# Buffers and load distances around a retention stage: three tiles for weight sums, longer prefetch, two shuffle tiles, masked keys on ScalarE

## The chip, the cores and the metric

The kernel runs on one core of one Trainium2 chip. The metric is the device time of one execution in microseconds (us); the number given for a kernel is the median of its runs. TensorE is called PE here (PEld is its weight load), VectorE DVE, ScalarE ACT, GpSimd POOL, and SyncE SP. SP computes nothing in this kernel; it issues the loads, in the order of its queue. POOL computes a little and issues the stores and a few loads.

## The reference

One step of a one-layer decoder over 1024 prompt tokens and 8 x 4 sample tokens, all in float32. The parts that matter here are the combined input projection, the retention branch with four heads, and its gate and output projection.

```python
h = xn @ w_in
q_a, k_a, v_a, q_r, k_r, v_r, gate_r, gm_a, gm_r = jnp.split(h, split_points(), axis=-1)
...
qr = rope_ret(q_r.reshape(B, T, N_HEADS_R, DK_R).astype(jnp.float32), pos)
kr = rope_ret(k_r.reshape(B, T, N_HEADS_R, DK_R).astype(jnp.float32), pos) * (DK_R ** -0.5)
o_r, new_s = retention(qr, kr, vr, ret_s0.astype(jnp.float32))
y_r = (jax.nn.silu(gate_r) * head_rms(o_r)) @ w_r_proj
mixed = (jax.nn.sigmoid(gm_a) * y_a + jax.nn.sigmoid(gm_r) * y_r) @ w_o
x = x + rms_norm(mixed, g_post_mix)
f, new_conv = conv_ffn(rms_norm(x, g_pre_ffn), conv_ctx, w_up, conv_w, conv_b, w_down)

def retention_chunk(q, k, v, s0, log_g):     # one block of 128 tokens (4 for a sample row)
    scores = jnp.einsum('bihd,bjhd->bhij', q, k) * dmask[None]
    inner = jnp.einsum('bhij,bjhe->bihe', scores, v)
    cross = jnp.einsum('bihd,bhde->bihe', q, s0) * q_decay[None, :, :, None]
    s_new = (jnp.exp(log_g * L)[None, :, None, None] * s0
             + jnp.einsum('bjhd,bjhe->bhde', k * k_decay[None, :, :, None], v))
    return inner + cross, s_new
```

## The kernel before

Every float32 product is made of three matmuls on a high and a low part of each operand (`mm3`, L254 to L257). The high part is a copy by ACT (L228, L329), the low part a subtraction by DVE (L223, the line of the helper `ew`, through which most of DVE's arithmetic goes). The large products use a seven-product scheme on 2 x 2 blocks, so that sums of weight blocks have to be made: by DVE for the input weights in `in_split`, and, for two later matrices, ahead of their use in `quad_sums`, which loads a piece of `w_down` or `w_r_proj` into a tile `zt`, makes four sums in place and stores the tile to DRAM (`s_d`, `r_d`).

The stage that the change touches lies at about 270 to 740 us. Its backbone is `stream()`, a generator that runs 16 pairs of column blocks of the input projection through PE (PSUM tiles `ps_q`), each pair in two halves of tokens (`j`), each half of seven products of 12 matmuls. Between the products other work is put in by hand, by `adv(n)`, which lets the stream run n products further:

- **The sample part**, about 320 to 455 us: `sample(h)` for the four heads. For each pair of sample rows it loads a state `s0`, splits it (`s0s`), multiplies the keys by a mask of one row (`kb`, L1039, two for each pair of rows, 32 in all) and updates the state. In the same time `post_qk` turns q and k of the heads by their angles: a shuffle on DVE into a tile `sh` (L822), a product on POOL, a product and a sum (all L223 or L225).
- **The prompt part**, about 455 to 715 us: 32 blocks of retention (4 heads of 8 blocks). `ahead(g)` issues the loads of q and k (`qk`, by SP, L1089) and of v (`vt`, by POOL, L1096) of a later block and makes the block's scores (`front`, L1118, L1119). `middle` multiplies by v and moves the state on (L1131 to L1138), `tail` multiplies by the gate, and in the first three blocks of each head calls `quad_sums`; in blocks 4 and 7 `z_sums` makes four sums of the gated result into another `zt` tile. `post_ga` loads a `zt` tile too (L838).

The tiles `zt` are two and turn around between these three users; the weights of a pair lie in two tiles `w_raw` of three, two in a pool `wraw` and one in a pool `wsum`. A tile whose turn comes again makes its writer wait until the last use of its old content has ended. A scheduler sets the order on each engine when the program is built; each engine and each queue then works in that order.

Of the kernel before, what the change touches and what calls it, by code (L numbers as in the profile page):

```python
# [120 lines left out]
def trunk(ctx, tc, I, O):  # L121
# [95 lines left out]
    def f32(ap):  # L217
        return ap.bitcast(F32)
# [63 lines left out]
        G.tensor_tensor(out=rs[:r, :c], in0=ms[:r, :c], in1=mhalf[:r, :c], op=ALU.pow)  # L282
        return rs[:r, :c]

    def quad_sums(w, d, m, pt, kk, q, eng=None):
        eng = eng or V


        q = q[:, :, :2 * P]
        for u in range(2):  # L290
            r0, c0 = 1024 * pt + 512 * kk, (m + 4 * u) * P
            pin(ld.dma_start(out=q[:, :, u * P:u * P + P],
                             in_=w[r0:r0 + 512, c0:c0 + P].rearrange("(k p) n -> p k n", p=P)))
        a11, a12, a21, a22 = (q[:, r::2, u * P:u * P + P] for u in range(2) for r in range(2))
        ew(eng, a22, a21, a22, add)
        ew(V, a21, a11, a21, sub)
# [4 lines left out]
    def down_sums(n, q, eng=None):  # L301
        quad_sums(w_down, s_d, n // 6, n // 2 % 3, n % 2, q, eng)

    def quad_weights(raw, w, d, p, c, pt):

# [511 lines left out]
    def post_qk(h):  # L817
        def post(j, o):
            c, d = (t[:, 2 * HW * j:2 * HW * (j + 1)] for t in (rcos, rsin))
            for i in range(2):  # L820
                sh, x = ST("sh", (P, 2 * HW)), both(o)[:, i]
                V.stream_shuffle(sh, x, R_SHUF)  # L822
# [4 lines left out]
        return post  # L827

    def post_gate(h):
        def post(j, o):  # L830
            S.activation(o, o, AF.Silu)
            st.dma_start(out=of_half(gr_d[h], j), in_=both(o))
        return post

    def post_ga(m):
        def post(j, o):
            y = ST("zt", (P, T), bufs=2)
            ld.dma_start(out=both(y), in_=of_half(gm_d[m:m + 2], j))  # L838
            S.activation(o, o, AF.Sigmoid)
            ew(V, o, o, y, mult)  # L840
            st.dma_start(out=of_half(a_d[m:m + 2], j), in_=both(o))
        return post

    def post_gm(m):
        def post(j, o):
            st.dma_start(out=of_half(gm_d[KD + m:KD + m + 2], j), in_=both(o))
        return post
# [8 lines left out]

    def in_split(n):

        a11, a12, a21, a22 = pair_weights(w_in, *pairs[n][:2])
        yield  # L860
        s1 = wx["sum"].tile([P, 4, P], F32, name="s1")
        yield w_split(a11, V)
        ew(V, s1, a21, a22, add)
        yield w_split(s1, V)
        ew(V, s1, s1, a11, sub)
        yield w_split(s1, V)
        yield w_split(a12, V)
        ew(V, a12, a12, s1, sub)
        yield w_split(a12, V)
        ew(V, a21, a11, a21, sub)  # L870
        yield w_split(a21, V)
        yield w_split(a22, V)

    def stream():

        early = (A11, S1, S2, A12, S4, S3)
        ws = in_split(ORDER[0])
        next(ws)
        ops = {p: next(ws) for p in early}
        coming = in_split(ORDER[1])  # L880
# [2 lines left out]
        for i, n in enumerate(ORDER):  # L883
            for j in range(2):
# [17 lines left out]
                for p in (A11, S1, A22, S2, A12, S4, S3):  # L902
                    if p == A22:
                        if last is not None:
                            product(A22, *last)
                        if j == 0:
                            ops[A22] = next(ws)
                            ws = coming
                        if last is not None:
                            yield  # L910
                        continue
                    if p == S2:
                        if nh < 2:
                            TE.matmul(bk[1], ops[p][:, 0], xop(ex1, p, j, 0)[0], start=True, stop=True)
                            S.copy(out=bk[1], in_=bk[0])
                        nh += 1
                    product(p, bk[{A11: 0, A12: 0, S2: 1, S3: 1, S1: 2, S4: 2}[p]], ops[p], j, dst)
                    if p == A11 and nh >= 2:
                        S.copy(out=bk[1], in_=bk[0])
                    if p == S4:  # L920
                        V.tensor_tensor(out=c12, in0=bk[2], in1=c12, op=add)
                    if p == S3:
                        V.tensor_tensor(out=c22, in0=bk[1], in1=c22, op=add)
# [9 lines left out]
                PEND.append((pairs[n][2], j, o))  # L933
            if i + 1 < len(ORDER):
                ops = nxt
        product(A22, *last)
# [53 lines left out]
    def load_s0(n):  # L990
        if n >= 2 * DB:
            return
        h, bb = n // 4, 2 * (n % 4)
        s0s_[n] = ST("s0", (P, 2, 256), bufs=3)
        ld.dma_start(out=s0s_[n], in_=I["state_ret"][0, bb:bb + 2, h].rearrange("b k e -> k b e"))

    def sample(h):
        gS = float(GAMMA[h] ** 4)
        dm = ST("dm", (P, P))
        ld.dma_start(out=dm, in_=I["dmask"][:, h, 1])  # L1000
        qk8 = ST("qk8", (P, 2, NS), bufs=2)
# [24 lines left out]
        TE.matmul(po, h8[:, 0, 0:2 * NS], v8, start=True, stop=False)  # L1026
        for bb in range(0, DB, 2):
            s0 = s0s_[(h * DB + bb) // 2]
            load_s0((h * DB + bb) // 2 + 1)
# [6 lines left out]
            pk = ps_a()  # L1036
            for b in range(2):
                kb = ST("kb", (P, P), F32R, bufs=2)
                V.tensor_scalar(out=kb, in0=f32(h8)[:, 1], scalar1=bm[:, bb + b:bb + b + 1],  # L1039
                                scalar2=None, op0=mult)  # L1040
                TE.matmul(pk[:, 256 * b:256 * b + 256], kb, v8, start=True, stop=True)
            V.scalar_tensor_tensor(out=s0, in0=s0, scalar=gS,
                                   in1=pk.rearrange("p (b e) -> p b e", b=2), op0=mult, op1=add)
# [102 lines left out]
    def tail(g, pt, o):  # L1146
# [3 lines left out]
        while a < NS + P * tt + P:  # L1150
# [561 lines left out]
```

## Time and profile before

| | |
|---|---|
| Median of 3 runs | 1695.76 us (1694.22 to 1698.17) |
| Profiled execution, its own time | 1696.89 us |
| Its span, first to last instruction | 1695.1 us |
| Mean granted clock of PE | 0.993 |
| PE busy | 1637.6 us |
| DVE busy | 1227.7 us |
| ACT busy | 852.1 us |
| POOL busy | 485.2 us |

The times run from the span's start. A matmul's row in the profile is longer than its turn, as matmuls overlap, so a PE that is busy all the time is only a PE without gaps. In a row of groups stand the line, the engine, the operation, the tile written and those read, the count, then the busy time, the mean time of one in ns, and the idle time of the engine just before them with what ended it. In a row of waits stand the waiting engine and line, what it waited for, the total in us, how many times, and the longest. In a row of stretches stand, for each engine, the busy time and the number of instructions, and then the granted clock of PE (1.00 is full), the busy share of the DMA engines and GB/s.

### The profile page before, as it was taken

How to read it: one execution, taken by the hardware profiler on the slowest of the kernel's cores; microseconds unless marked ns; L12 is line 12 of the kernel's file. 1: busy time of each engine (PE TensorE's matmuls, PEld its weight loads, DVE VectorE, ACT ScalarE, POOL GpSimd, SP SyncE). 2: the span in 40 equal slices, each digit the busy share in tenths (PEclk: the TensorE clock that was granted, in tenths of full speed). 3: DMA queues.
4: the chain of work that ended last, by engine and by line, in shares of the span. 5: the costliest groups of instructions: out<-in, count | busy, mean ns of one | idle time of the engine just before them, and what ended most of it. 6: DMA issues, size and time to landing. Idle time of an engine off the chain costs nothing.

```text
span 1695.1 us, 32482 instructions
## 1 busy us (share of the span) xinstructions
PE 1637.6 (97%) x12551; PEld 1593.2 (94%) x12551; DVE 1227.7 (72%) x2067; ACT 852.1 (50%) x1858; POOL 485.2 (29%) x686
## 2 busy tenths in 40 slices
PE   8999999888989999999999999999999999999997
PEld 7999989887979999999778999999999999999997
DVE  7887737798545666557756888888888888445576
ACT  6566534444545554454432555555555556443343
POOL 4242420455233433232311123222222323111102
PEclk9999999999999999999999999999999999999998
DMA  7212222444666777497722245444444447866654
GB/s 197 66 45 73 80 76 103 138 144 146 218 200 198 243 233 248 156 294 223 227 98 83 69 132 158 146 154 149 157 156 145 145 146 251 251 185 201 199 170 160
DMA packets 273291, 273.88 MB, mean 162 GB/s; under 512 B 23041, under 2 KB 234273, under 8 KB 273122
## 3 DMA queue, kind: packets, MB, share of 16 engines
q1 hardware_dynamic: 239377, 155.25, 31.6%
q0 software_dynamic: 33760, 116.57, 19.8%
q8 instruction: 98, 1.61, 0.4%
q14 instruction: 56, 0.45, 0.1%
HBM read 184.24 MB, written 87.49 MB: 160 GB/s over the span
## 4 chain that ended last, share of the span: by engine, by line
PE 62%; DMA 5%; DVE 4%; issue 3%; ACT 1%; POOL 1%; SPq 0%; DVEq 0%; POOLq 0%; ACTq 0%
PE ps_m L257 9%; PE ps_m L255 9%; PE ps_m L256 9%; PE ps_t L256 8%; PE ps_t L255 7%; PE ps_t L257 7%; PE ps_q L255 3%; PE ps_q L257 3%; PE ps_q L256 3%; DMA zt<-in_w_down 1%; DMA a_in<-a_d 1%; PE ps_b L1131 1%; DMA qk<-qk_d 1%; PE ps_a L1135 0%; PE ps_t L459 0%
## 5 line engine op out<-in xcount | busy, mean ns | idle before, releaser
L255 PE MATMUL ps_q<-xh,w 128*128 128x264 f32 x512 | 153.2, 299 | 9.4 <-ACT pair L900 6.2
L223 DVE SCALAR_TENSOR_TENSOR w_lo<-w_raw,w_hi 128x1024 fp32r<-128x1024 f32 x83 | 104.4, 1264 | 61.8 <-ACT w_hi L228 57.6
L255 PE MATMUL ps_t<-xh,w_hi 128*128 128x264 f32 (+2 forms) x524 | 148.9, 284 | 0.0
L256 PE MATMUL ps_t<-xl,w_hi 128*128 128x264 f32 (+2 forms) x524 | 148.7, 284 | 0.0
L257 PE MATMUL ps_t<-xh,w_lo 128*128 128x264 f32 (+2 forms) x524 | 148.0, 283 | 0.0
L256 PE MATMUL ps_q<-xl,w 128*128 128x264 f32 x512 | 147.2, 288 | 0.0
L257 PE MATMUL ps_q<-xh,w 128*128 128x264 f32 x512 | 146.5, 287 | 0.0
L257 PE MATMUL ps_m<-xh,w_lo 128*128 128x264 f32 x512 | 145.5, 285 | 0.7 <-DVE w_lo L223 0.7
L255 PE MATMUL ps_m<-xh,w_hi 128*128 128x264 f32 x512 | 145.9, 285 | 0.0
L256 PE MATMUL ps_m<-xl,w_hi 128*128 128x264 f32 x512 | 145.5, 284 | 0.0
L223 DVE SCALAR_TENSOR_TENSOR w<-w_raw,w 128x512 fp32r<-128x512 f32 x152 | 106.7, 707 | 36.1 <-ACT w L329 33.6
L1462 DVE SCALAR_TENSOR_TENSOR c_out<-u_ext,fconst,c_out 128x1024 f32<-128x1024 f32 x96 | 121.8, 1280 | 2.6 <-ACT c_out L1458 0.5
L228 ACT CAST w_hi<-w_raw 128x1024 fp32r<-128x1024 f32 x62 | 65.2, 1051 | 100.8 <-PE ps_t L256 73.6
L255 PEld LDWEIGHTS ps_q<-xh,w 128*128 128x128 f32 x512 | 97.6, 191 | 11.8 <-ACT pair L900 6.8
L329 ACT CAST w<-w_raw 128x512 fp32r<-128x512 f32 x152 | 93.8, 621 | 28.3 <-DVE w_raw L223 13.2
L257 PEld LDWEIGHTS ps_t<-xh,w_lo 128*128 128x128 f32 x524 | 98.7, 188 | 0.0
L256 PEld LDWEIGHTS ps_t<-xl,w_hi 128*128 128x128 f32 x524 | 98.6, 188 | 0.0
L255 PEld LDWEIGHTS ps_t<-xh,w_hi 128*128 128x128 f32 x524 | 98.6, 188 | 0.0
L256 PEld LDWEIGHTS ps_q<-xl,w 128*128 128x128 f32 x512 | 97.6, 191 | 0.6
L257 PEld LDWEIGHTS ps_q<-xh,w 128*128 128x128 f32 x512 | 97.2, 190 | 0.1
L257 PEld LDWEIGHTS ps_m<-xh,w_lo 128*128 128x128 f32 x512 | 96.3, 188 | 1.1 <-DVE w_lo L223 1.0
L255 PEld LDWEIGHTS ps_m<-xh,w_hi 128*128 128x128 f32 x512 | 96.3, 188 | 0.2
(448 smaller groups left out, 6059.9 us busy)
## 6 DMA issues: line engine op xcount, KB each, us to landing
w_raw<-in_w_up SPq DMA_DIRECT2D x48, 512.0 KB, 4.3
w_raw<-in_w_in SPq DMA_DIRECT2D x42, 512.0 KB, 4.3
w_raw<-s_d SPq DMA_DIRECT2D x60, 256.0 KB, 3.8
t_d<-t POOLq DMA_DIRECT2D x24, 528.0 KB, 3.9
t<-t_d POOLq DMA_DIRECT2D x24, 528.0 KB, 5.2
t<-in_w_down SPq DMA_DIRECT2D x40, 256.0 KB, 4.6
s_d<-t POOLq DMA_DIRECT2D x20, 512.0 KB, 3.5
w_raw<-in_w_down SPq DMA_DIRECT2D x36, 256.0 KB, 5.7
```

The lines of the kernel that those rows point to most:

```text
L223: pinned(V.scalar_tensor_tensor(out=out, in0=in0, scalar=1.0, in1=in1, op0=mult, op1=op))
L228: pinned(S.copy(out=hi, in_=src))
L255: TE.matmul(ps, wh, xh, start=start, stop=False, **kw)
L256: TE.matmul(ps, wh, xl, start=False, stop=False, **kw)
L257: TE.matmul(ps, wl, xh, start=False, stop=stop, **kw)
L329: S.copy(out=t[:, 0:4], in_=src)
L1131: TE.matmul(po, sT, vt, start=True, stop=tt == 0)
L1462: V.scalar_tensor_tensor(out=c[:, NS:], in0=u[:, g, NU + t:NU + t + SEQ], scalar=sc[t], in1=c[:, NS:], op0=mult, op1=add)
```

## The change

Six things are done:

1. `quad_sums` is cut in two. `quad_load` issues the loads of a piece in the `tail` of blocks 0, 1 and 2 of a head; the sums and the store are made in the `tail` of the block after (1, 2 and 3). The tiles `zt` become three. `post_ga` issues its load as soon as a half is ready and not when its other work is done.
2. `qk` is loaded 4 blocks ahead into 5 tiles (2 ahead into 3 before), `vt` 3 ahead into 5 (2 into 4), the states `s0` 2 ahead into 4 (1 into 3).
3. `post_qk` has two shuffle tiles and makes both shuffles first.
4. The masked keys `kb` are made on ACT.
5. The third `w_raw` tile leaves the pool `wsum`: in the sample part the weights have two tiles, in the prompt part again three. The two loads of a pair are issued apart, the second when the pair before has made its last split.
6. The multiplication of the gate by the sample's result moves from `gate` to the `tail` of a head's first block.

```diff
-    def quad_sums(w, d, m, pt, kk, q, eng=None):
-        eng = eng or V
+    def quad_load(w, m, pt, kk, q):
         q = q[:, :, :2 * P]
         for u in range(2):
             r0, c0 = 1024 * pt + 512 * kk, (m + 4 * u) * P
             pin(ld.dma_start(out=q[:, :, u * P:u * P + P], ...
+    def quad_sums(d, m, pt, kk, q, eng=None):
...
-    wx["sum"] = wx["raw"] = pool("wsum", 1, stack=sm_stack)
+    wx["sum"], wx["raw"] = pool("wsum", 1, stack=sm_stack), wraw
...
+            sh = [ST("sh", (P, 2 * HW), bufs=2) for _ in range(2)]
             for i in range(2):
-                sh, x = ST("sh", (P, 2 * HW)), both(o)[:, i]
-                V.stream_shuffle(sh, x, R_SHUF)
+                V.stream_shuffle(sh[i], both(o)[:, i], R_SHUF)
+            for i in range(2):
+                x = both(o)[:, i]
                 ew(G, x, x, c, mult)
-                ew(V, sh, sh, d, mult)
-                ew(G, x, x, sh, add)
+                ew(V, sh[i], sh[i], d, mult)
+                ew(G, x, x, sh[i], add)
...
-        def post(j, o):
-            y = ST("zt", (P, T), bufs=2)
-            ld.dma_start(out=both(y), in_=of_half(gm_d[m:m + 2], j))
+        def post(j, o, y):
             S.activation(o, o, AF.Sigmoid)
             ew(V, o, o, y, mult)
             st.dma_start(out=of_half(a_d[m:m + 2], j), in_=both(o))
+        def begin(j, o):
+            y = ST("zt", (P, T), bufs=3)
+            ld.dma_start(out=both(y), in_=of_half(gm_d[m:m + 2], j))
+            return lambda: post(j, o, y)
...
-        a11, a12, a21, a22 = pair_weights(w_in, *pairs[n][:2])
-        yield
+        r = []
+        for c in pairs[n][:2]:
+            NRAW[0] += 1
+            p = wx["raw"] if NRAW[0] % 3 == 0 else wraw
+            r.append(p.tile([P, KD, P], F32, name="w_raw", tag="raw"))
+            ld.dma_start(out=r[-1], in_=w_in[:, c:c + P].rearrange("(k p) n -> p k n", p=P))
+            yield
...
                             ops[A22] = next(ws)
                             ws = coming
+                            if i + 1 < len(ORDER):
+                                next(ws)
...
-        s0s_[n] = ST("s0", (P, 2, 256), bufs=3)
+        s0s_[n] = ST("s0", (P, 2, 256), bufs=4)
...
-                V.tensor_scalar(out=kb, in0=f32(h8)[:, 1], scalar1=bm[:, bb + b:bb + b + 1],
-                                scalar2=None, op0=mult)
+                S.mul(kb, f32(h8)[:, 1], bm[:, bb + b:bb + b + 1])
...
-    rp = pool("rp", 1, stack=ph_stack)
+    wx["raw"] = rp = pool("rp", 1, stack=ph_stack)
...
+        QS = [(w_r, r_d, h, 0, 0), (w_r, r_d, h, 0, 1), (w_down, s_d, 3, (20 + h) // 2 % 3, h % 2)]
         if tt < 3:
-            q_ = quarters(ST("zt", (P, T), bufs=2))
-            down_sums(20 + h, q_) if tt == 2 else quad_sums(w_r, r_d, h, 0, tt, q_)
+            quads[h, tt] = quarters(ST("zt", (P, T), bufs=3))
+            w, _, *at = QS[tt]
+            quad_load(w, *at, quads[h, tt])
+        if 0 < tt < 4:
+            quad_sums(*QS[tt - 1][1:], quads.pop((h, tt - 1)))
...
-        load_qk(g + 2)
-        load_v(g + 2)
+        load_qk(g + 4)
+        load_v(g + 3)
```

The scheduler makes another order of it. The instructions of PE are the same in number; DVE has 32 fewer and ACT 32 more. Three places show it.

DVE, in the first sample head, before. `sh` is the shuffle tile, `kb` the masked keys, `s0s` the split state, `w` and `s` parts and sums of the input weights, and `s` with `ps_a` a state; digits behind a name number its buffer:

```order
L1021 TENSOR_TENSOR h_3918<-t_3915,h_3918 64x256
L822 STREAM_SHUFFLE sh<-pair 128x528
L923 TENSOR_TENSOR pair<-ps_q_3818,pair 128x264
L1039 TENSOR_SCALAR kb<-h_3918,bm 128x128 x2
L223 SCALAR_TENSOR_TENSOR sh<-sh,rsin 128x528
L1039 TENSOR_SCALAR kb<-h_3918,bm 128x128
L223 SCALAR_TENSOR_TENSOR s0s<-s_3972,s0s 128x512
L1042 SCALAR_TENSOR_TENSOR s_3562<-s_3562,ps_a 128x512
L1039 TENSOR_SCALAR kb<-h_3918,bm 128x128
```

The same place now:

```order
L1036 TENSOR_TENSOR h_3920<-t_3917,h_3920 64x256
L937 TENSOR_TENSOR pair<-ps_q_3817,pair 128x264
L223 SCALAR_TENSOR_TENSOR s_3969<-w_raw 128x512
L824 STREAM_SHUFFLE sh<-pair 128x528
L223 SCALAR_TENSOR_TENSOR w_raw<-w_raw 128x512
L939 TENSOR_TENSOR pair<-ps_q_3818,pair 128x264
L223 SCALAR_TENSOR_TENSOR sh<-sh,rsin 128x528
L1056 SCALAR_TENSOR_TENSOR s_3562<-s_3562,ps_a 128x512
```

The masked keys are gone from DVE's row; what stood behind them moves up, and the state update (L1042, now L1056) no longer stands between them.

SP's queue where the prompt part begins, before. `z` is a gate tile, `zt<-in_w_r_proj` and `zt<-in_w_down` are the loads for the sums:

```order
L1105 DMA z<-gr_d 128x2x528
L340 DMA w_raw<-in_w_in 128x8x128
L1089 DMA qk<-qk_d 128x2x128 x3
L1105 DMA z<-gr_d 128x2x528
L340 DMA w_raw<-in_w_in 128x8x128
L1089 DMA qk<-qk_d 128x2x128 x2
L292 DMA zt<-in_w_r_proj 128x4x128 x2
L1089 DMA qk<-qk_d 128x2x128
L292 DMA zt<-in_w_r_proj 128x4x128 x2
```

The same place now:

```order
L1120 DMA z<-gr_d 128x2x528
L1104 DMA qk<-qk_d 128x2x128 x5
L871 DMA w_raw<-in_w_in 128x8x128 x2
L1104 DMA qk<-qk_d 128x2x128
L871 DMA w_raw<-in_w_in 128x8x128
L1120 DMA z<-gr_d 128x2x528
L1104 DMA qk<-qk_d 128x2x128
L289 DMA zt<-in_w_r_proj 128x4x128 x2
L1104 DMA qk<-qk_d 128x2x128
```

Five loads of q and k stand together ahead of the weights of the next pair, where three stood behind one of them.

DVE in blocks 3 to 5 of the first head, before. `zt<-zt` are sums of weights, `zt<-z` and `zt<-z,zt` those of the gated result, `sT` the scores of a block and `state` its state:

```order
L223 SCALAR_TENSOR_TENSOR zt<-zt 128x2x128 x2
L1138 SCALAR_TENSOR_TENSOR state<-state,ps_a 128x256
L223 SCALAR_TENSOR_TENSOR zt<-zt 128x2x128
L223 SCALAR_TENSOR_TENSOR w7x<-w_raw,w7x 128x512
L223 SCALAR_TENSOR_TENSOR zt<-zt 128x2x128
L1154 TENSOR_TENSOR z<-ps_b,z 128x2x112
L1154 TENSOR_TENSOR z<-ps_b,z 128x2x16
L1121 TENSOR_TENSOR sT<-ps_a,dm 128x128
```

The same place now:

```order
L223 SCALAR_TENSOR_TENSOR zt<-zt 128x2x128
L223 SCALAR_TENSOR_TENSOR w_5827<-w_raw,w_5827 128x512
L223 SCALAR_TENSOR_TENSOR zt<-zt 128x2x128
L1166 TENSOR_TENSOR z<-ps_b,z 128x2x112
L223 SCALAR_TENSOR_TENSOR w_5860<-w_raw,w_5860 128x512
L1166 TENSOR_TENSOR z<-ps_b,z 128x2x16
L223 SCALAR_TENSOR_TENSOR zt<-zt 128x2x128
L223 SCALAR_TENSOR_TENSOR zt<-z 128x264 x2
L1133 TENSOR_TENSOR sT<-ps_a,dm 128x128
L223 SCALAR_TENSOR_TENSOR zt<-zt 128x2x128
L223 SCALAR_TENSOR_TENSOR zt<-z,zt 128x264 x2
```

The sums of `w_down` (`zt<-zt`) stand one block later, among those of the gated result, which have a tile of their own.

More of the change, by code (lines that the diff above doesn't have):

```diff
@@ L293, in quad_sums @@
                              in_=w[r0:r0 + 512, c0:c0 + P].rearrange("(k p) n -> p k n", p=P)))
+    def quad_sums(d, m, pt, kk, q, eng=None):
+        eng = eng or V
+        q = q[:, :, :2 * P]
         a11, a12, a21, a22 = (q[:, r::2, u * P:u * P + P] for u in range(2) for r in range(2))
         ew(eng, a22, a21, a22, add)
-        ew(V, a21, a11, a21, sub)
+        ew(eng, a21, a11, a21, sub)
         ew(eng, a11, a22, a11, sub)
@@ L299, in quad_sums, with down_sums @@
         st.dma_start(out=d[m, pt, :, 4 * kk:4 * kk + 4], in_=q)
-    def down_sums(n, q, eng=None):
-        quad_sums(w_down, s_d, n // 6, n // 2 % 3, n % 2, q, eng)
+    def down_sums(n, q):
+        quad_load(w_down, n // 6, n // 2 % 3, n % 2, q)
+        quad_sums(s_d, n // 6, n // 2 % 3, n % 2, q)
     def quad_weights(raw, w, d, p, c, pt):
@@ L832, in post @@
             st.dma_start(out=of_half(gr_d[h], j), in_=both(o))
-        return post
+        return lambda j, o: lambda: post(j, o)
     def post_ga(m):
-        def post(j, o):
-            y = ST("zt", (P, T), bufs=2)
-            ld.dma_start(out=both(y), in_=of_half(gm_d[m:m + 2], j))
+        def post(j, o, y):
             S.activation(o, o, AF.Sigmoid)
@@ L841, in post @@
             st.dma_start(out=of_half(a_d[m:m + 2], j), in_=both(o))
-        return post
+        def begin(j, o):
+            y = ST("zt", (P, T), bufs=3)
+            ld.dma_start(out=both(y), in_=of_half(gm_d[m:m + 2], j))
+            return lambda: post(j, o, y)
+        return begin
     def post_gm(m):
@@ L846, in post @@
             st.dma_start(out=of_half(gm_d[KD + m:KD + m + 2], j), in_=both(o))
-        return post
+        return lambda j, o: lambda: post(j, o)
     pairs = [(QR0 + P * h, KR0 + P * h, post_qk(h)) for h in range(4)]
@@ L857, in in_split @@
     def in_split(n):
-        a11, a12, a21, a22 = pair_weights(w_in, *pairs[n][:2])
-        yield
+        r = []
[5 more added lines that the diff above has]
+            yield
+        a11, a12, a21, a22 = r[0][:, 0:4], r[0][:, 4:8], r[1][:, 0:4], r[1][:, 4:8]
         s1 = wx["sum"].tile([P, 4, P], F32, name="s1")
@@ L908, in stream @@
                             ws = coming
+                            if i + 1 < len(ORDER):
+                                next(ws)
                         if last is not None:
@@ L932, in stream @@
                 last = bk[1], ops[A22], j, dst
-                PEND.append((pairs[n][2], j, o))
+                PEND.append(pairs[n][2](j, o))
             if i + 1 < len(ORDER):
@@ L947, in flush @@
         while PEND:
-            post, j, o = PEND.pop(0)
-            post(j, o)
+            PEND.pop(0)()
     rcos, rsin = ST("rcos", (P, T)), ST("rsin", (P, T))
@@ L1000, in sample @@
         ld.dma_start(out=dm, in_=I["dmask"][:, h, 1])
-        qk8 = ST("qk8", (P, 2, NS), bufs=2)
+        qk8 = ST("qk8", (P, 2, NS))
         ld.dma_start(out=qk8, in_=qk_d[h].rearrange("i p t -> p i t")[:, :, :NS])
@@ L1028, in sample @@
             s0 = s0s_[(h * DB + bb) // 2]
-            load_s0((h * DB + bb) // 2 + 1)
+            load_s0((h * DB + bb) // 2 + 2)
             s0s = ST("s0s", (P, 2, 2, 256), F32R)
@@ L1049, in sample @@
         S.copy(out=z8[:, h], in_=turn(pt, finish(os8, NS, 1, h, 1)))
-    load_s0(0)
+    for n in range(2):
+        load_s0(n)
     adv(18)
@@ L1069, in z_sums @@
         b11, b12, b21, b22 = (z[:, HW * i:HW * i + HW] for i in range(4))
-        t1, t2, t3, t4 = (q[:, i] for q in (quarters(ST("zt", (P, T), bufs=2)),) for i in range(4))
+        t1, t2, t3, t4 = (q[:, i] for q in (quarters(ST("zt", (P, T), bufs=3)),) for i in range(4))
         ew(V, t1, b12, b11, sub)
@@ L1080, in z_sums @@
         st.dma_start(out=z_d[h, :, 2, j], in_=b22)
-    zlast, gts, qks, vts, state, NBLK = [], {}, {}, {}, {}, 4 * NB
+    zlast, gts, qks, vts, state, quads, NBLK = [], {}, {}, {}, {}, {}, 4 * NB
     def load_qk(g):
@@ L1087, in load_qk @@
         h, tt = divmod(g, NB)
-        qks[g] = ST("qk", (P, 2, P), bufs=3)
+        qks[g] = ST("qk", (P, 2, P), bufs=5)
         ld.dma_start(out=qks[g], in_=qk_d[h].rearrange("i p t -> p i t")[:, :, cols(tt)])
@@ L1094, in load_v @@
         h, tt = divmod(g, NB)
-        vts[g] = ST("vt", (P, 256), bufs=4)
+        vts[g] = ST("vt", (P, 256), bufs=5)
         st.dma_start(out=vts[g], in_=v_d[h, tt])
@@ L1105, in gate @@
         ld.dma_start(out=both(t), in_=of_half(gr_d[h], j))
-        if j == 0:
-            g = both(t)[:, :, 0:NS]
-            V.tensor_tensor(out=g, in0=g, in1=z8[:, h], op=mult)
         gts[h, j] = t
@@ L1155, in tail @@
             a = b
+        if tt == 0:
+            g_ = both(gts[h, 0])[:, :, 0:NS]
+            V.tensor_tensor(out=g_, in0=g_, in1=z8[:, h], op=mult)
+        QS = [(w_r, r_d, h, 0, 0), (w_r, r_d, h, 0, 1), (w_down, s_d, 3, (20 + h) // 2 % 3, h % 2)]
         if tt < 3:
-            q_ = quarters(ST("zt", (P, T), bufs=2))
-            down_sums(20 + h, q_) if tt == 2 else quad_sums(w_r, r_d, h, 0, tt, q_)
+            quads[h, tt] = quarters(ST("zt", (P, T), bufs=3))
[3 more added lines that the diff above has]
+            quad_sums(*QS[tt - 1][1:], quads.pop((h, tt - 1)))
         if tt in (4, NB - 1):
@@ L1188, in ahead @@
             state["dm"] = mask(g // NB)
-        load_qk(g + 2)
-        load_v(g + 2)
+        load_qk(g + 4)
+        load_v(g + 3)
         return front(g, state["dm"])
-    for g in range(2):
+    for g in range(4):
         load_qk(g)
+    for g in range(3):
         load_v(g)
@@ L1211, in trunk @@
     for n in range(4):
-        load_z(n, quarters(ST("zt", (P, T), bufs=2)) if n < 2 else TT("z_raw", (P, 4, HW)))
+        load_z(n, quarters(ST("zt", (P, T), bufs=3)) if n < 2 else TT("z_raw", (P, 4, HW)))
     for _ in STR:
```

2 lines of the change are left out of this document (1 added, 1 removed).

## The prediction

> **What bounds the kernel now.** I read the page first (busy times, then the slices), then the stretches around the changed stage, then PE's waits there, and last what DVE, SP and the clock do at each wait.
>
> ```profile
> span 1695.1 us, 32482 instructions
> PE 1637.6 (97%) x12551; PEld 1593.2 (94%) x12551; DVE 1227.7 (72%) x2067; ACT 852.1 (50%) x1858; POOL 485.2 (29%) x686
> PE   8999999888989999999999999999999999999997
> DVE  7887737798545666557756888888888888445576
> ```
>
> PE is busy for 97% of the span, so time can be won only where PE has gaps. One slice is 42.4 us; slices 8 to 10 and 12 (297 to 424 and 466 to 508 us, counting from 1) are under 90%, and in the first three of them DVE stands at 7, 9 and 8 tenths. The stretches say how much:
>
> ```profile
> core 0: us, PE busy (x) PEld busy (x) DVE busy (x) ACT busy (x) POOL busy (x), PEclk, DMA share, GB/s
> 300.00:320.00 20.00, 17.13 (x132) 16.40 (x132) 13.15 (x21) 6.76 (x18) 7.44 (x7) 1.00 0.55 180
> 320.00:420.00 100.00, 86.51 (x673) 82.50 (x674) 94.49 (x160) 40.96 (x105) 59.41 (x48) 1.00 0.43 139
> 460.00:520.00 60.00, 49.68 (x327) 47.46 (x327) 28.28 (x64) 24.56 (x65) 18.03 (x31) 0.89 0.67 211
> 520.00:620.00 100.00, 99.81 (x767) 97.52 (x766) 59.64 (x131) 57.46 (x142) 35.96 (x60) 1.00 0.74 229
> 620.00:640.00 20.00, 18.17 (x140) 17.46 (x138) 13.76 (x32) 10.34 (x26) 9.38 (x15) 1.00 0.79 253
> ```
>
> Between 320 and 420 us DVE is the bound: busy 94.49 of 100, PE 86.51. Between 460 and 520 no engine is: PE 49.68 of 60 and DVE 28.28, so PE waits for something that comes late. From 520 on PE has no gaps but one at 620 to 640; 99.81 us for 767 matmuls make 0.130 us for one. PE's waits from 300 to 520 us (what waits, for what, total us, times, longest):
>
> ```profile
> PE ps_q L255 <- ACT pair L900: 6.2, 2, 4.9
> PE ps_a L1041 <- DVE kb L1039: 5.5, 6, 1.4
> PE ps_a L1118 <- DMA qk<-qk_d: 5.0, 2, 2.7
> PE ps_q L255 <- DVE pair L921: 3.2, 3, 1.2
> PE ps_q L255 <- DVE pair L923: 2.1, 2, 1.9
> PE ps_b L1035 <- DVE s0s L223: 2.1, 3, 1.4
> ```
>
> The masked keys, the additions to `pair` and `s0s` are all DVE's work of the sample part. The 4.9 us behind ACT's copy and the 5.0 us for `qk` belong to the prompt part's start. Rows of the chain and of DVE's timeline there:
>
> ```profile
> 454.88 8.61 DMA qk<-qk_d
> 490.76 5.43 DMA zt<-in_w_down
> 496.28 0.89 DVE L223 SCALAR_TENSOR_TENSOR zt<-zt 128x256 f32<-128x256 f32 x2 [5.04 <-DMA zt<-in_w_down]
> 499.07 5.91 DMA s_d<-zt
> 505.07 0.78 DVE L223 SCALAR_TENSOR_TENSOR zt<-z 128x264 f32<-128x264 f32 x2 [3.36 <-DMA s_d<-zt]
> 507.46 0.59 PE ps_q L255
> 625.92 1.34 DVE L223 SCALAR_TENSOR_TENSOR zt<-zt 128x256 f32<-128x256 f32 x3 [4.20 <-DMA zt<-in_w_down]
> ```
>
> DVE works in order. It stands 5.04 us for a weight block still on its way, then 3.36 us because `z_sums` wants a `zt` tile whose store has not landed; behind it stands the addition to `pair`, behind that ACT's copy of it, and PE restarts at 507.46. At 625.92 a load of `w_down` is late again. After the stalls the clock falls:
>
> ```profile
> 464.50:467.90 3.40, 3.40 (x18) 3.40 (x17) 1.13 (x4) 0.62 (x2) 0.00 (x0) 0.50 0.89 295
> 495.20:498.60 3.40, 3.14 (x14) 3.17 (x15) 2.29 (x6) 0.00 (x0) 0.00 (x0) 0.50 0.71 204
> 505.40:512.20 6.80, 4.74 (x21) 4.74 (x22) 3.54 (x8) 2.05 (x6) 4.03 (x7) 0.50 0.84 305
> ```
>
> Three stretches at half clock hold 3.40 + 3.14 + 4.74 = 11.28 us of PE's work, which would take 5.64 less at full clock.
>
> **The change part by part.** *Masked keys on ACT, two shuffle tiles.*
>
> ```profile
> L1039 DVE TENSOR_SCALAR kb<-h,bm x32: 264/281/1348, 334.7 to 444.5; 128x128 fp32r<-128x128 f32 x32
> L1018 ACT ACTIVATE t<-ps_a,kdec 128x128 f32<-128x128 f32 x4 | 1.5, 364 | 4.5 <-DVE t L1017 4.5
> L1039 DVE TENSOR_SCALAR kb<-h,bm 128x128 fp32r<-128x128 f32 x32 | 16.5, 526 | 0.0
> 320.00:420.00 100.00, 7.03 (x23) 4.31 (x23) 14.14 (x24) 1.00 0.43 139
> POOL pair L225 <- DVE sh L822: 18.4, 13, 3.0
> DVE sh L822 <- POOL pair L225: 4.0, 2, 2.6
> ```
>
> The fourth row is the stretch of 320 to 420 us for the tile `kb` alone (PE, PEld, DVE). DVE gives up 32 operations, 16.5 us, a mean of 526 ns against a fastest of 264 and a median of 281: some are held up to 1348 ns. On ACT the nearest operation, the same 128x128 multiplied by a column, takes 364 ns: 32 x 0.364 = 11.6 us on an engine busy 40.96 of 100, so I cost it at nothing; if that cover went, `kb` would wait in ACT's row behind the copies of `ps_q`, and PE's six waits would name ACT. The shuffles lose a wait of 4.0 us on DVE for the single tile. In 320 to 420 DVE gives up 14.14 of its 94.49, which leaves 80.35, under PE's 86.51: DVE ceases to be the bound. Most PE can then win is its idle time, 100 - 86.51 = 13.5 us (16.4 with the 2.87 of 300 to 320); the least is the 5.5 us that name `kb`, or nothing if another wait fills them. I take the middle of 5.5 and 13.5, **9.5 us**, since 80 of some 90 still leaves DVE little room to be on time.
>
> [...]
>
> *The third `w_raw` tile leaves the sample part; the loads of a pair are issued apart.*
>
> ```profile
> DVE s L223 <- DMA w_raw<-in_w_in: 6.3, 4, 2.8
> w_raw<-in_w_in SPq DMA_DIRECT2D x42, 512.0 KB, 4.3
> SPq L340 <- DVE w L223: 61.3, 9, 33.1
> ```
>
> DVE already waits for these loads, 6.3 us in four waits from 300 to 460 us, and no wait of PE names what it makes then. The second load of a pair can now be issued only when the pair before has split its A22, in its first half; DVE wants it about six products later, and 72 matmuls x 0.130 are 9.4 us at least, against 4.3 us to land. PE wants the result a product row later still. What SP waits for here (L340, up to 33.1 us) holds back everything behind it in its queue, the loads of `s0` among them, which is why these are issued two ahead. Bounds: nothing, or the whole landing in each of six pairs, 6 x 4.3 = 25.8 us of loss. I charge **-2**, a third of the 6.3 that DVE waits already, near the lower end because PE waits for none of it today.
>
> *`qk`, `vt` and `s0` further ahead.* The additional loads are none; they are only earlier. At 463 and 495 us PE waits 5.0 us for `qk`; with five loads ahead of the weights in SP's queue both should go. *`quad_sums` a block later, three `zt` tiles.* A load has a block longer to land, so the waits of 5.04 and 4.20 go; the 3.36 goes because the tile of the last store isn't the next one. The stalls go over to SP, whose row waits for the store in DVE's stead; `qk` stands behind it, but four blocks ahead. *The gate's product* moves 4 operations to another place in DVE's row, under a microsecond each where DVE is half idle: nothing, hidden by PE's work of a block.
>
> Price of these three together: PE's idle time in 460 to 520, 60 - 49.68 = 10.32, and 5.64 for the clock make 15.96. Least: 4, if the waits on `qk` are simply replaced and only the one behind `zt` (4.9) goes. I take **12**: the stretch also holds small waits that nothing here touches. At 620 to 640 PE idles 1.83, of which I take **1.5**.
>
> The clock goes by stalls in these rows, and all three followed ones of 2.5 to 5.2 us. [...]
>
> *Sum.* 9.5 + 12 + 1.5 - 2 = 21.0. The profiled execution took 1696.89, so 1675.9; it stands 1.13 above the median of the runs, hence **1674.8**, rounded to 1675.
>
> **The rivals.**
>
> R1, *DVE stays slow*. The hold-ups of `kb` beside POOL pass to the next DVE operation, so only 24 x 0.281 = 6.7 us leave DVE, its idle time stays, and the first term is 6.7. And with one tile fewer DVE's wait for `w_raw` doubles, 6.3 of loss in place of 2. 6.7 + 12 + 1.5 - 6.3 = 13.9, **1682**. For it speaks the spread of `kb`; against it that PE had no wait for `w_raw`.
>
> R2, *the prompt part keeps its stalls*. SP waits for the stores of `zt` with the weights and `qk` queued behind it, and PE's wait comes back under the name `qk` or `w_raw`. The 12 falls to 0: **1687**. For it: SP waits already (61.3 us in nine); against it: loads stand four blocks ahead.
>
> R3, *slower*. With two tiles each pair's second load is exposed: it is issued late and lands behind `qk` and `s0` in the queue. It decides if queueing and landing together exceed the 9.4 us to DVE and then the slack to PE. 25.8 lost in place of 2: **1699**. Against it: a landing of 4.3.
>
> R4, *nothing moves*. The order is new, but other DVE work fills each gap in the sample part (9.5 goes) and R2 holds besides; with 1.5 - 2 left this is **1696**.
>
> R5, *everything goes*: 2.87 + 13.5 + 15.96 + 1.83 = 34.1, **1662**; it needs a DVE that is never late, and two tiles that cost nothing.
>
> **How the numbers follow.** The forecast 0.45, R1 0.20, R2 0.11, R3 0.08, R4 0.06, R5 0.10. The range runs from R5 to a little past R2, 1662 to 1688; it leaves out R3 and R4 and, as each case has some spread of its own, about as much again at its two ends. A measurement of this kernel can tell about 0.2%, 3.4 us, from no change. The forecast, R1, R2 and R5 are faster by more: 0.86; R4 is the same, some of R2's upper end with it: 0.07; slower: 0.07.
>
> **What would show each step.** Right: in the sample part DVE under 88 of 100 and PE over 93; no wait of PE on `kb` over 1 us in all, whether it names DVE or ACT; DVE operations of 1.3 us and more beside POOL's show R1 instead. Between blocks 0 and 4 of the first head no wait of DVE on `s_d<-zt` or `in_w_down`, none of PE on `qk`, and the clock at 1.00 throughout. SP's waits on the store of `zt` and on `w_raw` grow; if PE waits on `w` or `s1` parts behind a `w_raw` load, R3 is at work. The prediction is wrong if PE's idle time in the sample part remains near 13 with new names, or if a stall at the start of the prompt part halves the clock again.

## The result, and the profile after

The changed kernel takes 1675.12 us (median of 4 runs, 1673.30 to 1678.56), the kernel before 1695.55 in the same series: a ratio of 0.9887, interval 0.9872 to 0.9901. That is 20.4 us less, where 21 were forecast. The profiled execution took 1678.56, so it is the slowest of the four and 3.4 above their median; its span is 1676.8. A second profile of the same kernel, taken with the first group of experiments, has a span of 1673.0. Both are used below, since stages differ by some 2 us from one to the other.

From the page of the first, and its stretches in the columns shown before (PE, PEld, DVE, ACT, POOL, clock, DMA):

```profile
span 1676.8 us, 32469 instructions
PE 1630.4 (97%) x12551; PEld 1587.5 (95%) x12551; DVE 1221.8 (73%) x2035; ACT 861.5 (51%) x1890; POOL 485.0 (29%) x686
PE   8999999899999999999999999999999999999997
DVE  7887738699566566558757988888888888455476
```

```profile
300.00:320.00 20.00, 16.72 (x131) 16.18 (x132) 13.47 (x22) 7.19 (x18) 8.21 (x7) 1.00 0.66 221
320.00:420.00 100.00, 90.25 (x715) 86.71 (x715) 93.95 (x144) 52.34 (x142) 60.84 (x50) 1.00 0.48 148
460.00:520.00 60.00, 58.44 (x445) 56.70 (x445) 36.39 (x81) 32.94 (x82) 23.77 (x40) 1.00 0.75 238
520.00:620.00 100.00, 97.94 (x746) 95.10 (x745) 62.11 (x136) 56.52 (x137) 37.85 (x62) 1.00 0.79 251
620.00:640.00 20.00, 20.00 (x158) 19.68 (x158) 11.73 (x25) 10.27 (x27) 8.08 (x14) 1.00 0.71 219
```

PE's gaps at 460 to 520 us are nearly gone (58.44 of 60, after 49.68), with the clock at 1.00 where it was 0.89. But from 320 to 420 DVE is as busy as before, 93.95 of 100, with 144 operations in place of 160, and PE still idles for nearly 10 us. PE's waits from 300 to 520 us:

```profile
PE ps_b L1050 <- DVE s0s L223: 4.9, 7, 0.8
PE ps_q L255 <- DVE pair L939: 3.4, 2, 1.7
PE ps_q L255 <- ACT pair L914: 2.3, 2, 1.3
PE ps_q L255 <- DVE pair L937: 1.8, 2, 1.5
PE ps_b L1143 <- issue: 1.2, 1, 1.2
```

No wait on `kb`, none on `qk`, none of 4.9 us behind ACT. What is left in the sample part is DVE under other names: `s0s` had 2.1 us and has 4.9.

To place gains I use one figure for each stage: how much earlier than the kernel before PE has done the same amount of its work (each matmul weighted by its undisturbed distance to the next), worked out from PE's records. The marks are times of the kernel before; a minus is a gain. "Half clock" is the time from 300 to 760 us at a granted clock of 0.5. In the kernel before, matmuls of 264 columns start 0.22 us apart in it (464.6 to 467.8 us) and 0.12 apart at full clock (520 to 620 us), so nearly half of the time that PE works in it is lost.

| kernel | ratio, 95% interval | 300-455 (sample) | 455-520 | 520-620 | 620-640 | half clock |
|---|---|---|---|---|---|---|
| before | 1 | 0 | 0 | 0 | 0 | 13.6 |
| changed, first profile | 0.9887 (0.9872 to 0.9901) | -6.8 | -13.3 | +3.8 | -2.3 | 0 |
| changed, second profile | 0.9898 (0.9881 to 0.9916) | -6.1 | -14.1 | +2.2 | -2.2 | 3.4 |
| kb back on DVE | 0.9925 (0.9905 to 0.9944) | +1.3 | -12.6 | +3.3 | -2.4 | 10.2 |
| kb on ACT alone | 0.9950 (0.9932 to 0.9967) | +0.9 | -13.2 | -0.3 | +2.0 | 20.5 |
| POOL's turning cut | 0.9832 (0.9807 to 0.9858) | -19.1 | -14.2 | +2.7 | -2.3 | 0 |
| zt undone (edit 1) | 0.9910 (0.9897 to 0.9922) | -8.3 | -11.7 | +1.8 | +1.7 | 6.8 |
| qk, vt undone (of edit 2) | 0.9890 (0.9875 to 0.9905) | -7.9 | -10.6 | +4.1 | -2.4 | 6.8 |
| both undone | 0.9898 (0.9885 to 0.9912) | -7.0 | -12.6 | +1.9 | 0.0 | 3.4 |
| one shuffle tile | 0.9905 (0.9892 to 0.9919) | -1.5 | -13.8 | +3.2 | -2.4 | 6.8 |
| w_raw alone (edit 5) | 0.9987 (0.9972 to 1.0003) | -0.4 | -3.1 | +1.7 | -0.3 | 10.2 |
| kb on ACT and w_raw | 0.9951 (0.9936 to 0.9967) | +0.5 | -11.7 | +1.7 | +2.2 | 17.1 |
| sample spread | 0.9970 (0.9957 to 0.9982) | -8.7 | -11.6 | +6.9 | -1.5 | 10.2 |
| sample later | 0.9962 (0.9948 to 0.9977) | -5.6 | -11.3 | +3.8 | -2.4 | 6.8 |

The ratios come from 4 to 12 timed runs each, the stages from one profile each. A single profile holds 0 to 20.5 us of half clock (last column), in the sample part and at the start of the prompt part, so a difference of 2 us between two stage figures says little.

### The profile page after: what moved, and what is told of

The parts are those of the page before. It is cut to its first block, busy times and chain, and to the rows that moved or that the text cites. A ratio compares the mean times of both kernels' runs of the same rounds, so it can differ in the third digit from the quotient of the medians.

```text
span 1676.8 us, 32469 instructions
## 1 busy us (share of the span) xinstructions
PE 1630.4 (97%) x12551; PEld 1587.5 (95%) x12551; DVE 1221.8 (73%) x2035; ACT 861.5 (51%) x1890; POOL 485.0 (29%) x686
## 4 chain that ended last, share of the span: by engine, by line
PE 64%; DMA 4%; DVE 4%; issue 3%; ACT 1%; POOL 1%; SPq 0%; DVEq 0%; POOLq 0%; ACTq 0%
PE ps_m L257 9%; PE ps_m L256 9%; PE ps_m L255 9%; PE ps_t L256 7%; PE ps_t L255 7%; PE ps_t L257 7%; PE ps_q L255 4%; PE ps_q L257 4%; PE ps_q L256 4%; DMA zt<-in_w_down 1%; DMA t<-z_d 1%; PE ps_b L1143 1%; PE ps_a L1147 1%; DVE xl L223 1%; PE ps_b L1145 1%
## 5 line engine op out<-in xcount | busy, mean ns | idle before, releaser
L223 DVE SCALAR_TENSOR_TENSOR w<-w_raw,w 128x512 fp32r<-128x512 f32 x152 | 110.4, 733 | 37.3 <-ACT w L331 36.0
L255 PEld LDWEIGHTS ps_q<-xh,w 128*128 128x128 f32 x512 | 96.4, 188 | 5.9 <-ACT pair L914 2.8
L223 DVE SCALAR_TENSOR_TENSOR xl<-t,xh 128x1056 fp32r<-128x1056 f32 (+1 forms) x53 | 67.7, 1281 | 40.5 <-ACT xh L228 40.3
```

The costliest lines, as they stand in the source:

```text
L223: pinned(V.scalar_tensor_tensor(out=out, in0=in0, scalar=1.0, in1=in1, op0=mult, op1=op))
L255: TE.matmul(ps, wh, xh, start=start, stop=False, **kw)
```

## The experiments

**1. Who bounds the sample part.** Four kernels; the first is the changed kernel unaltered.

> The changed kernel as it is, so that the others of this group have it on the same chip, and for a second profile. All theories: 1673 to 1677. In the first profile DVE's own row of operations from 300 to 448 us was busy 133.2 us, of which 26.7 us lay above the fastest tenth of each form; the same is expected within 1 us.

1677.72 us, just above the range. The time of DVE's operations above the fastest tenth of their form, called hold-ups here, summed to 28.7 us from 300 to 448 us, not within 1 of 26.7: the hold-ups themselves vary by 2 us.

The second puts the masked keys back:

```diff
-                S.mul(kb, f32(h8)[:, 1], bm[:, bb + b:bb + b + 1])
+                V.tensor_scalar(out=kb, in0=f32(h8)[:, 1], scalar1=bm[:, bb + b:bb + b + 1],
+                                scalar2=None, op0=mult)
```

> The changed kernel with the masked keys back on DVE. Theory A (DVE bounds the sample part, and the hold-up beside POOL passes from one DVE operation to the next): DVE gets 32 more operations of 0.28 us, some 9 us, plus little more hold-up in all (26.7 us stay 25 to 30, spread over more operations), and with no room in the sample part most of it shows: 1680 to 1684. Theory B (the masked keys bring their hold-ups with them): kb's mean is 0.5 us and the other forms keep their means, 32 x 0.53 = 17 us more on DVE, 1686 to 1690. Theory C (the two shuffle tiles and the new order made the gain of the sample part): within 2 us of 1675.

1681.78 us, 4.1 more than the unaltered kernel of the same group; the ratios' intervals meet. DVE's groups from 300 to 460 us of this kernel, then the same two of the changed kernel (first profile):

```profile
L1054 DVE TENSOR_SCALAR kb<-h,bm 128x128 fp32r<-128x128 f32 x32 | 18.5, 588 | 0.3 <-PE ps_a L1056 0.2
L223 DVE SCALAR_TENSOR_TENSOR w<-w_raw,w 128x512 fp32r<-128x512 f32 x25 | 19.9, 804 | 2.0 <-ACT w L331 2.0
L223 DVE SCALAR_TENSOR_TENSOR sh<-sh,rsin 128x528 f32<-128x528 f32 x16 | 14.2, 892 | 1.3 <-DMA rsin<-in_rsin 1.3
```

```profile
L223 DVE SCALAR_TENSOR_TENSOR w<-w_raw,w 128x512 fp32r<-128x512 f32 x25 | 23.9, 976 | 4.4 <-ACT w L331 4.2
L223 DVE SCALAR_TENSOR_TENSOR sh<-sh,rsin 128x528 f32<-128x528 f32 x16 | 17.9, 1121 | 1.8 <-DMA rsin<-in_rsin 1.6
```

With `kb` on DVE it takes 588 ns each, of which some 280 are its own (its median was 281 in the kernel before); without it, the parts `w` go from 804 to 976 and the products `sh` from 892 to 1121. The hold-ups, 28.8 us with `kb` on DVE and 26.7 and 28.7 without, pass from one operation to the next (theory A); theory B, where they leave with `kb`, is out. One hold-up of the changed kernel (first profile), on DVE and on POOL:

```profile
322.67 1.83 DVE L223 SCALAR_TENSOR_TENSOR w<-w_raw,w 128x512 fp32r<-128x512 f32 x1
322.17 1.78 POOL L225 TENSOR_TENSOR pair<-pair,rcos 128x528 f32<-128x528 f32 x1 [4.99 <-DVE sh L824]
```

DVE's operation begins while POOL's runs and ends 0.55 us after it. So it is throughout this profile: 29 of POOL's 32 products and sums each held up one DVE operation by over 0.25 us, and each of the 29 ended 0.05 to 0.58 us after POOL's operation. In the kernel before there were 28 such hold-ups, and 29 with `kb` back on DVE: in all three nearly as many as POOL's 32 operations, with `kb` on DVE or not.

The third is the kernel before with the same line of `kb` on ACT and no other edit.

> The kernel before with the masked keys on ACT and nothing else. Theory A: DVE's 144.7 us of the sample part fall by 9 to 11, the sum of the hold-ups falls from 28.0 by 1 or 2 only, and the time by 5 to 8: 1688 to 1691. Theory B: 17 us less on DVE and 10 to 13 us less in time: 1683 to 1686. Theory C: within 2 us of 1695.5.

1685.51 us, 8.5 less by its ratio: more than A expected. The sum of DVE's operations fell by 8.1 us (144.7 to 136.6) and the hold-ups did not fall at all (27.9 to 28.8), as in A, but the time did not come from the sample part. In this profile that part gained nothing, with 13.7 us of it at half clock, some 6 us of loss as estimated from the distances of 0.22 and 0.12 us. The gain is the 13.2 us of the next stage, which nobody expected of `kb`; experiments 2 and 3 follow that.

The fourth leaves out most of the turning of q and k on POOL:

```diff
-                ew(G, x, x, c, mult)
+                ew(G, x[:, :8], x[:, :8], c[:, :8], mult)
...
-                ew(G, x, x, sh[i], add)
+                ew(G, x[:, :8], x[:, :8], sh[i][:, :8], add)
```

> The changed kernel with POOL's product and sum in the turning of q and k done on 8 of 528 columns; the other columns of q and k are left unturned. Theory A: the 26.7 us of hold-ups on DVE fall under 6, DVE is no longer the bound of the sample part (133 falls to about 107 us of 148), PE's idle time there (some 18 us with the small gaps) mostly goes: 1658 to 1664. Rival (PE's gaps there come of chains of dependences, not of DVE's load): the hold-ups go and PE's gaps stay, 1670 to 1675.

1664.72 us, just above A's range. The same two groups of DVE, the stretch, and PE's largest waits of 300 to 520 us:

```profile
L223 DVE SCALAR_TENSOR_TENSOR w<-w_raw,w 128x512 fp32r<-128x512 f32 x26 | 17.5, 688 | 4.9 <-ACT w L331 4.7
L223 DVE SCALAR_TENSOR_TENSOR sh<-sh,rsin 128x528 f32<-128x528 f32 x16 | 11.2, 706 | 0.8 <-DMA rsin<-in_rsin 0.7
320.00:420.00 100.00, 97.68 (x796) 96.29 (x795) 76.21 (x151) 61.80 (x162) 30.77 (x54) 1.00 0.51 164
PE ps_q L255 <- ACT pair L914: 1.5, 2, 1.3
PE ps_q L255 <- DVE pair L939: 1.1, 1, 1.1
```

The hold-ups fell from 28.7 to 1.7 us, DVE to 76.21 of 100, and PE's gaps went with them: the sample part gained 19.1 us, 12 to 13 more than the whole change did there. So in the changed kernel it is still DVE's load that makes PE's gaps, over a fifth of it hold-ups beside POOL. (POOL's own results also came earlier here; that part was not separated, but no wait of PE names POOL.)

**2. What cured the start of the prompt part.** Four kernels from the changed one: edit 1 undone (two `zt` tiles, sums beside their loads), edit 2 undone for `qk` and `vt` (the states `s0` stay 2 ahead in 4 tiles), both undone, and for the sample part one shuffle tile.

```diff
-            quad_load(w, *at, quads[h, tt])
-        if 0 < tt < 4:
-            quad_sums(*QS[tt - 1][1:], quads.pop((h, tt - 1)))
+            quad_load(w, *at, quads[h, tt])
+            quad_sums(*QS[tt][1:], quads.pop((h, tt)))
...
-        load_qk(g + 4)
-        load_v(g + 3)
+        load_qk(g + 2)
+        load_v(g + 2)
```

> The changed kernel with two zt tiles, the sums of weights in the same block as their loads, and post_ga's load late, as before. Theory P (the prediction: the sums a block later take away DVE's waits of 5.0, 3.4 and 4.2 us and PE's stalls behind them): the stall behind ACT's copy of pair at the start of the prompt part (4.9 us, and about 2.4 for the clock) and the one at 628 us (1.6) come back, 1682 to 1686. Theory O (at the start of the prompt part it is the place of the waiting sums in DVE's row that makes a stall or not, and the masked keys on ACT alone moved it): DVE waits for the loads as before, PE does not stall behind them, 1675 to 1679.

1679.81 us. PE's waits from 440 to 640 us, and the stretch around the first:

```profile
PE ps_q L255 <- ACT pair L911: 3.3, 1, 3.3
PE ps_b L1140 <- issue: 1.8, 1, 1.8
484.00:488.00 4.00, 0.71 (x5) 0.47 (x5) 3.14 (x7) 0.56 (x3) 2.20 (x5) 1.00 1.03 357
488.00:492.00 4.00, 4.00 (x31) 3.90 (x31) 1.31 (x4) 1.05 (x5) 2.05 (x5) 1.00 1.10 355
```

Two stalls of the kernel before are back, smaller: 3.3 us at 488 (4.9 before) and 1.8 at 608. By the ratios (0.9910 against 0.9898 and 0.9887, with intervals that meet) the undoing costs some 2 to 4 us, between P and O.

> The changed kernel with q and k loaded 2 ahead into 3 tiles and v 2 ahead into 4. Theory P: PE's waits for qk (2.5 and 2.9 us, and about 3.4 for the clock) come back, 1682 to 1686, with SP's row showing qk behind the waits for zt and w_raw. Theory O: at most one of them comes back, 1676 to 1680.

1676.37 us: no cost. PE waited 4.2 us for `state` in five waits of up to 2.0 between 440 and 640 us, and not once for `qk`. O.

> Both of the former undone together; masked keys on ACT, two shuffle tiles, two w_raw tiles in the sample part and loads of a pair apart remain. Theory P: the whole 13 us of the prompt part's start come back and the 2 at 628 us, 1687 to 1691. Theory O: as the kernel before with masked keys on ACT alone, which had one stall of 2.7 us there, 1677 to 1682.

1677.86 us, and a ratio equal to that of the unaltered kernel, 0.9898. No wait of PE on `qk`, none behind a store. P is out: without edits 1 and 2 the stage from 455 to 520 us still gains 12.6 of its 13.3 to 14.1.

> The changed kernel with one shuffle tile and each shuffle just ahead of its products. Theory A (DVE's load and the hold-ups bound the sample part): DVE's wait for the tile of 4 us comes back, half of it on the bound, 1676 to 1680, and the hold-ups stay near 27 us. Rival (with the shuffles first POOL starts its product earlier, which is worth more than the tile): 1680 or more.

1679.75 us, some 1 to 3 more than with two tiles by the ratios, whose intervals overlap; the hold-ups were 27.0, as A says. DVE's wait for the tile came back at 1.4 us, not 4. The sample part gained 1.5 instead of 6 to 7 in this profile, of which up to 3 (6.8 us of half clock at the same distances) went to half clock after a stall of 3.5 us at 392; the tile's own worth is not settled beyond that.

**3. The queue, and an attempt at more.** Edit 5 alone and edits 4 and 5, both on the kernel before; then the changed kernel with the sample part thinned or begun later.

> The kernel before with edit 5 alone: two w_raw tiles in the sample part, the loads of a pair issued apart. Theory Q (the stalls at the prompt part's start come from SP's queue: a load of w_raw stood ahead of the first loads of q and k and waited 10.6 us for DVE): the first qk are issued before 447 us (454.9 before), no wait of PE on qk near 463, and the later stalls move with it: 1683 to 1690, with the sample part as before within 2 us. Theory D (only a lighter DVE cures them): 1693 to 1697. Rival R3 of the prediction (two tiles expose each load): over 1700, with DVE waiting for w_raw over 20 us from 300 to 455.

1690.85 us, between the ranges of Q and D, and a ratio of 0.9987 whose interval holds 1. SP's queue of the kernel before, then of this one, and PE's waits of this one from 455 to 520 us:

```profile
454.42 0.37 SPq L340 DMA_DIRECT2D w_raw<-in_w_in  x1
454.88 3.59 SPq L1089 DMA_DIRECT2D qk<-qk_d  x3
```

```profile
437.72 2.78 SPq L1098 DMA_DIRECT2D qk<-qk_d  x3
440.61 13.04 SPq L864 DMA_DIRECT2D w_raw<-in_w_in  x2
PE ps_a L1127 <- DMA qk<-qk_d: 4.0, 1, 4.0
PE ps_q L255 <- ACT pair L907: 4.0, 1, 4.0
```

Q holds for the first stall alone: the loads of q and k no longer stand behind a weight load that waits for DVE, they go out 17.2 us earlier, and the stall at 463 is gone. The other two stand, at 4.0 and 4.0 us. The prediction's rival R3 is out: DVE waited 7.2 us for `w_raw` from 300 to 455, near the 6.3 of the kernel before.

> The kernel before with edits 4 and 5: masked keys on ACT and w_raw as after. Theory Q with A: the prompt part's start is cured (13 us), the sample part gains 1 to 3 without the second shuffle tile: 1678 to 1682, so that edits 1 and 2 are worth nothing beside them. If edits 1, 2 or 6 do carry something: 1684 or more.

1684.58 us, no better than `kb` alone (0.9951 and 0.9950), so the first expectation missed. The start is cured (-11.7). Against the kernel that lacks only the second shuffle tile, 4.6 us are missing at 620 to 640, where edit 1 is absent, and 2.0 in the sample part, where 3.4 us more ran at half clock.

What carries the rest stays open. The kernel with edits 1 and 2 undone (0.9898) gains some 9 us more by the ratios than this one (0.9951). The two differ by edits 3 and 6, the earlier states `s0` of edit 2, and the tile `qk8` of the sample part, of which the change also makes one out of two. The second shuffle tile was worth 1 to 3 us; the others were undone in no run.

The two attempts at more, in one cut of code (the comments name the kernel that has the line):

```diff
-    adv(18)
+    adv(24)                        # sample later
...
-        for _ in sample(h):
-            adv(3)
+        for u, _ in enumerate(sample(h)):
+            adv(4 if u < 2 and h < 3 else 3)   # sample spread (with adv(18))
...
-    adv(len(ORDER) * 14 - 8 - 78 - 4 * NBLK - 1)
+    adv(len(ORDER) * 14 - 8 - 84 - 4 * NBLK - 1)   # both
```

> The changed kernel with six more products of the stream between the steps of the first three sample heads, taken from the nine that stand at the stream's end. Theory A (DVE bounds the sample part): the same DVE work beside 6 x 1.46 = 8.8 us more of PE's work, about half of which falls in today's gaps: 1668 to 1672. Rival (gaps are chains of a step, or the nine products at the end are needed there): 1675 to 1682.

> The changed kernel with the sample part begun six products of the stream later, the same six taken from the end. Theory A: the turning of q and k, with POOL's hold-ups, overlaps the sample part 6 products less of some 44, so 2 to 4 us of the 18 of gaps go: 1671 to 1674. Rival as for the spread: 1675 to 1682.

1687.90 and 1686.74 us: both slower than the changed kernel, beyond even the rival. PE's waits from 455 to 760 us with the spread:

```profile
PE ps_q L255 <- DVE pair L937: 4.6, 1, 4.6
PE ps_a L1130 <- DMA qk<-qk_d: 2.9, 1, 2.9
```

The sample part gained some 2 us more with the spread and none with the later start. Each then lost it three times: the first loads of q and k again stood behind a `w_raw` load in SP's queue (issued at 449 us, where the changed kernel issues them at 434) and PE waited 3 us at 460; a new stall of 3 to 5 us came at 551; and the end of the stage, short of six products, lost 3 to 4 (from the mark 640 to 755). No version faster than the changed kernel was found.

## Why the prediction came out right, and where its steps did not

The time (1675 against 1675.12) and the sizes by stage are near; two causes given for them did not hold as stated.

*The sample part: near in its sum by luck, wrong in its mechanism.* The forecast was 9.5 less 2; measured were 6.8 and 6.1. The step that failed is "DVE ceases to be the bound": it took the whole 14.14 us of `kb` off DVE. What left was the part that `kb` takes by itself, since the hold-ups passed on. This is rival R1's first term, 6.7, to within the spread. The signs set for it (DVE under 88, PE over 93) did not come: 93.95 and 90.25. The hold-ups ended just after POOL's operations, as shown above; their sum stays (28.8 with `kb` on DVE, 28.7 without), and it vanishes (1.7) when POOL's operations shrink. The charge of 2 for the third `w_raw` tile was too much, though DVE's wait for these loads about doubled, as R1 said, from 6.3 us between 300 and 460 us to

```profile
DVE s L223 <- DMA w_raw<-in_w_in: 12.4, 6, 5.0
```

(10.1 in the second profile): no wait of PE names what DVE makes of them, and edit 5 alone left the sample part as it was (-0.4). The two errors cancelled to about 1 us. ACT's `kb` took 397 ns where 364 was assumed, hidden as forecast.

*The start of the prompt part: right in size (12 forecast, 13.3 and 14.1 measured), wrong on what it takes.* The step that failed is "at 463 and 495 us PE waits 5.0 us for `qk`; with five loads ahead ... both should go", and with it "the waits of 5.04 and 4.20 go". With edits 1 and 2 undone the stalls stay away, so these edits are not needed for it. The size came right because it was read from PE's idle time and the clock there, which any cure gives back (the 5.64 for the clock is nearer 5.0 by the distances of 0.22 and 0.12 us). Moving `kb` to ACT alone does nearly all of it (13.2), although DVE still waits 4.95 us for `w_down` there. SP's and DVE's timelines of that kernel, and PE's one wait from 455 to 530 us:

```profile
446.71 2.79 SPq L1088 DMA_DIRECT2D qk<-qk_d  x3
483.90 0.42 DVE L923 TENSOR_TENSOR pair<-ps_q,pair 128x264 f32<-128x264 f32 x1
489.27 0.42 DVE L223 SCALAR_TENSOR_TENSOR zt<-zt 128x256 f32<-128x256 f32 x1 [4.95 <-DMA zt<-in_w_down]
490.22 1.33 DVE L223 SCALAR_TENSOR_TENSOR zt<-zt 128x256 f32<-128x256 f32 x3
496.70 0.77 DVE L223 SCALAR_TENSOR_TENSOR zt<-z 128x264 f32<-128x264 f32 x2
PE ps_a L1117 <- DMA qk<-qk_d: 2.6, 1, 2.6
```

The first `qk` go out 8.2 us earlier than before (454.88), in time for 463. An addition to `pair` stands just ahead of the long wait. And the sums of the gated result (`zt<-z`) begin 5.2 us after the last sum of `w_down` and wait for no store; in the kernel before they waited 3.36 us, with `pair` behind them. One stall of 2.6 us on `qk` remains. That these shifts of the rows, and not the lighter load by itself, are the cause was read from the traces and not tried apart. With `kb` back on DVE and the other edits in place the stage gains 12.6 too; so there are two sets of edits, each enough, and undoing either alone shows little. Whether edits 1 and 2 suffice by themselves was not run. Of the signs set for this part, PE without a wait on `qk`, DVE without one on a store, and the clock at 1.00 came true; but from 450 to 520 us DVE still waited 2.2 us for `w_down` and 3.1 for `w_r_proj`, with no wait of PE behind it.

*620 to 640 us: right.* 1.5 forecast, 2.3 and 2.2 measured, and the cause is edit 1: the five profiles of kernels without it show +2.2 to -0.3 there, those with it -1.5 to -2.4.

*520 to 620 us: not foreseen.* The gate's product and the moved sums were costed at nothing there. The stage lost 3.8 and 2.2 us; with edit 1 the kernels lose 2.2 to 6.9 there, without it at most 1.9. Waits from 520 to 640 us of PE, and of DVE to 560 us:

```profile
PE ps_a L1130 <- DVE state L1150: 2.0, 3, 1.1
DVE zt L223 <- DMA zt<-in_w_r_proj: 4.6, 1, 4.6
DVE zt L223 <- DMA zt<-in_w_down: 3.0, 1, 3.0
```

The step "a load has a block longer to land" was too simple: a block later it is still not always there. In the second head DVE waits 4.6 us for `w_r_proj` (4.0 before, at 520 to 580) and now 3.0 for `w_down` as well, and in the same stretch PE waits 2.0 for the state (0.6 before); that the one brings the other was not tried. Four of the five kernels without edit 1 lose 1.7 to 1.9 there as well; for that part the cause stays open.

*SP's queue.* As forecast its waits grew, and in the changed kernel no wait of PE came of it; from 230 to 740 us SP waited 61.3 us for these parts before, and after:

```profile
SPq L871 <- DVE w L223: 97.7, 11, 33.0
```

## What to carry to other kernels

DVE's hold-ups beside POOL summed to 28.8 us with `kb` on DVE and 28.7 without, and moving it saved DVE about its undisturbed time (8.1 us, where 32 x 281 ns are 9.0); with POOL's operations on 8 of 528 columns they summed to 1.7. Where a profile shows hold-ups like these, price an operation by its fastest duration, and look for the rest to the engine beside which it is slow. The stalls behind late loads went here with what stood behind the waiting instruction in its row; an edit elsewhere that reorders the row may remove such a stall, as `kb` seems to have done (13.2 us from 455 to 520), so before crediting a prefetch, undo the prefetch. When two edits each suffice, undoing one shows nothing: try each alone and both undone.

## What the hardware showed beside this

Between 300 and 760 us the kernel before ran at a granted clock of 0.50 three times, in the rows that the prediction shows: for 3.40 us from 464.50, for 3.40 from 495.20 and for 6.80 from 505.40. PE's waits there were 2.3 us, ended at 463.63, then 2.7, ended at 495.46, and 4.9, ended at 507.46; so the second and the third stretch at half clock began before the wait was over. A wait of 1.9 us that ended at 317.81 left the clock at 1.00.

The length of a wait did not decide it alone here. In the kernel with edit 1 undone PE waited 3.3 us at 488, longer than the 2.3 and 2.7 above, and the clock was 1.00 from 484 to 492 us (shown above). And one wait was not the same in two profiles of one kernel: PE's longest wait on `pair` (L939) took 1.7 us in the first profile of the changed kernel, with the clock at 1.00 from 300 to 420 us, and 3.1 in the second, which has this stretch:

```profile
319.60:323.00 3.40, 3.40 (x18) 3.40 (x17) 3.37 (x8) 1.75 (x6) 0.95 (x1) 0.50 0.06 10
```

Which waits bring half clock, and for how long, stays open. It makes one profile of a stage uncertain by a few microseconds, which is why the verdicts rest on timed runs where they can.
